# Gate and up weights: seven blocks, each in a tile of its own, split in the order of their products

## The chip, the cores and the metric

The kernel runs on one core of a Trainium2 chip. The metric is the device time of one execution in microseconds (us). Engines: TensorE (PE; its weight loads PEld), VectorE (DVE), ScalarE (ACT), GpSimd (POOL) and SyncE (SP, which issues the transfers).

## The reference

One layer of a hybrid decoder in fp32, on 1024 prompt positions and 64 sample positions (8 sequences of 8), 1088 columns in all:

```python
h = rms_norm(x, norm_mix_g)
proj = h @ w_in                       # convolution head group and dilated attention
x = x + concat([a, o]) @ w_out
h = rms_norm(x, norm_ffn_g)
g_full = concat([ffn_past, h @ w_ffn_gate])
g = depthwise_conv_valid(g_full, ffn_conv_w, ffn_conv_b)     # width 3
x = x + (silu(g) * (h @ w_ffn_up)) @ w_ffn_down
y = rms_norm(x, norm_final_g)
```

D_MODEL is 1024, D_FF is 2816. The change lies in the two products `h @ w_ffn_gate` and `h @ w_ffn_up`.

## The kernel before

Every matrix product is made exact by splitting both operands into a high part, which ACT writes by a copy that rounds to the matrix type, and a low part, the rest, which a subtraction writes (on POOL for the weights of this stage). Three matmuls then stand for one: high by high, high by low, low by high.

Gate and up are computed by a fast scheme for 2 x 2 blocks (Strassen and Winograd), seven products of blocks instead of eight. The inner dimension of 1024 is halved, the columns of h are halved (544 each), and a "weight" is a pair j of output tiles, j and j + 11, of 128 rows each. So a weight has four blocks of 128 x 512: a11 and a12 from the first output tile (raw tile g), a21 and a22 from the second (raw tile u), and four sums made of them:

- u2 = u1 + u2 gives s1, u1 = g1 - u1 gives s3, g1 = (new u2) - g1 gives s2, g2 = g2 - g1 gives s4. Here g1, g2, u1, u2 are halves of the raw tiles, and the sums (DVE, L945 to L948) are written in their place.

`products` multiplies the seven blocks with seven blocks of h (b11, t2, b21, t1, t3, b22, t4) in the order a11, s2, a12, s1, s3, s4, a22. Each product is 4 x 2 x 3 = 24 matmuls of 272 columns. Results accumulate in PSUM: px (a11, then a12), py (s2, then s1, then s4) and pz (s3, then a22). Between products DVE and ACT read them out: ta is a copy of px after a11, tb is py + ta, and `put` adds what belongs to each quarter of the result. So a later product on py has to wait for the sum read from it.

`ffn_pair(j)` does the gate of a pair, the width 3 convolution along columns (fc: one ACT and two DVE instructions per output tile, L1137 and L1139), the silu, then up, and u = up times the silu, which goes to DRAM in `ud`. There are eleven pairs; the first (gate0, up0) uses all eight products, without the scheme, while h is still being normalised, and takes its weights from splits of its own. Ten pairs, 20 weights, use the scheme.

Tiles for the weights of this stage:

- WR: two raw tiles of 1024 columns, filled by SP's transfers.
- WA: two tiles of 1024 columns, for the high and the low part of g (a11 and a12).
- W: five tiles of 1024 columns. `blocks_of_both` takes one for a22 (its high part in the left half, its low part in the right), two for s2 and s4 (high, low) and two for s3 and s1 (high, low).
- tmp: four tiles of 544 columns, used by ta and tb, and in the first pair by the sums that gate0 and up0 share.

What runs when is laid out by a planner at build time, from the order of the program, the free tiles and its own estimate of durations; at run time each engine goes through its instructions in the order laid out and waits where something is not ready.

After this stage, products with w_down follow (L172 to L174), which take their weights through the same WR and W tiles and read u back from DRAM.

Of the kernel before, what the change touches and what calls it, by code (L numbers as in the profile page):

```python
# [18 lines left out]
F32 = mybir.dt.float32  # L19
F32R = mybir.dt.float32r  # L20
AF = mybir.ActivationFunctionType
# [3 lines left out]
P = 128  # L25
D = 1024
# [38 lines left out]
HN = N // 2  # L65
# [12 lines left out]
def trunk_kernel(tc, xT, w_in, w_out, w_gate, w_up, w_down, par, kc, vc, sa, sf, pmask, smask,  # L78
                 yT, kT, vT, ca, cas, cf):
    nc = tc.nc  # L80
    with (
# [8 lines left out]
        def nm(s):  # L90
            cnt[0] += 1
            return f"{s}_{cnt[0]}"

        zone = {}
# [21 lines left out]
        def zt(z, tag, bufs, s, w=N, dt=F32):  # L116
            return zone[z].tile([P, w], dt, tag=tag, name=nm(s), bufs=bufs)

        def keep(s, w=N):
            return tp.tile([P, GW], F32, tag="T", name=nm(s))[:, :w]  # L120
# [143 lines left out]
        with ExitStack() as order:  # L264
            for k in range(KT):
                t = keep("x")
# [488 lines left out]
        i = 0  # L755
        for p in range(NS1, NP):
            prompt_heads(i, HEADS[p - NS1])
            i = HEADS[p - NS1]
# [55 lines left out]
        for p, upto in zip(range(NS1, NP), SHEADS):  # L814
            prompt_heads(i, upto)
            i = max(i, upto)
# [20 lines left out]
        def slot(tag, s, dt=F32R, w=HN):  # L837
            return zt("F", tag, 8, s, HN, dt)[:, :w]
# [43 lines left out]
        for h, tag in enumerate(("b11", "t2")):  # L882
            part.append([])
            for i in range(n):
                raw = slot("b11", "mx", F32)
                last_load = nc.sync.dma_start(raw, mixed[k0 + i][:, h * HN:h * HN + HN]).ins
                hi, lo = slot(tag, "mh"), slot(tag, "ml")
# [4 lines left out]
        for m0 in (0, 4):  # L892
            raw = wp.tile([P, D], F32, tag="WR", name=nm("wr"), bufs=WR)
            nc.sync.dma_start(raw.rearrange("p (m c) -> p m c", m=4),
                              w_out[m0:m0 + 4, :, k0 * P:].rearrange("m p c -> p m c"))
            for i in range(2):
                r = raw[:, i * 512:i * 512 + 512]
                hi, lo = slot("b21", "wh", w=512), slot("b21", "wl", w=512)
                nc.scalar.activation(hi, r, AF.Copy)
                nc.vector.tensor_sub(lo, r, hi.bitcast(F32))  # L900
                hi, lo = [t.rearrange("p (k c) -> p k c", c=P) for t in (hi, lo)]
# [14 lines left out]
        half = D // 2  # L916

        def weight_raw(w, j):
            raw = []
            for i in (j, j + HF):  # L920
                raw.append(wp.tile([P, D], F32, tag="WR", name=nm("wr"), bufs=WR))
                with tc.issue_after(last_load):
                    nc.sync.dma_start(raw[-1], w[i])
            return raw

        def weight_parts(x, new):
            n = x.shape[-1]
            hi, lo = new
            nc.scalar.activation(hi, x, AF.Copy)  # L929
            nc.gpsimd.tensor_sub(lo, x, hi.bitcast(F32))  # L930
            hi, lo = [t.rearrange("p (k c) -> p k c", c=P) for t in (hi, lo)]
            return [(hi[:, i:i + 4], lo[:, i:i + 4]) for i in range(0, n // P, 4)]

        def blocks_of_first(raw):
            return weight_parts(raw[0], [zt("F", "WA", 2, "wa", D, F32R) for _ in range(2)])

        def blocks_of_both(raw):
            def wide(s):
                return wp.tile([P, D], F32R, tag="W", name=nm(s))

            g, u = raw
            t = wide("w22")
            a22, = weight_parts(u[:, half:], (t[:, :half], t[:, half:]))
            g1, g2, u1, u2 = g[:, :half], g[:, half:], u[:, :half], u[:, half:]
            nc.vector.tensor_add(u2, u1, u2)  # L945
            nc.vector.tensor_sub(u1, g1, u1)
            nc.vector.tensor_sub(g1, u2, g1)
            nc.vector.tensor_sub(g2, g2, g1)  # L948
            s2, s4 = weight_parts(g, [wide("s24") for _ in range(2)])
            s3, s1 = weight_parts(u, [wide("s31") for _ in range(2)])  # L950
            return [a22, s1, s2, s3, s4]

        def weight_blocks(w, j):
            raw = weight_raw(w, j)
            return blocks_of_first(raw) + blocks_of_both(raw)


        raw = weight_raw(w_gate, 0)
        gate0 = blocks_of_first(raw) + weight_parts(raw[1], [wp.tile([P, D], F32R, tag="W", name=nm("wa"))
                                                             for _ in range(2)])  # L960
        raw = weight_raw(w_up, 0)
        up0 = []
        for i in range(2):
            up0 += weight_parts(raw[0][:, i * half:i * half + half], [slot("t4", "wa", w=half) for _ in range(2)])
        up0 += weight_parts(raw[1], [wp.tile([P, D], F32R, tag="W", name=nm("wa")) for _ in range(2)])


        x2d = [dp.tile([P, N], F32, name=f"x2d{m}") for m in range(KT)]
# [1 line left out]
        def out_half(h, hook):  # L970


            c = slice(h * HN, h * HN + HN)
            for m in range(KT):
                ps = pair()
                block_product(ps, wl[m], part[h], True)
                x = x2[m][:, c]
                added = nc.vector.tensor_add(x, all_of(ps), x).ins
                nc.sync.dma_start(x2d[m][:, c], x)
                s = slot("t1", "sq", F32)  # L980
                nc.scalar.activation(s, x, AF.Square)
                if m == 0:
                    acc = s
                else:
                    added = nc.vector.tensor_add(acc, s, acc).ins
                hook(m, added)
            return acc, added
# [8 lines left out]
        sq0, _ = out_half(0, lambda *_: None)  # L996
# [18 lines left out]
        def first_half(w, between=lambda: None, hook=lambda k, last: None):  # L1015

            a11, a12, a21, a22 = w
            o = pair("px"), pair("py")
            two_products(o, (a11, a21), blocks["b11"], True)
            shared = [zt("F", "tmp", 4, "ta", HN) for _ in o]  # L1020
            for t, ps in zip(shared, o):
                nc.scalar.activation(t, all_of(ps), AF.Copy)
            between()
            two_products(o, (a12, a22), blocks["b21"], False, hook)
            kept = [slot("t4", "c1", F32) for _ in o]
            for t, ps in zip(kept, o):
                nc.scalar.activation(t, all_of(ps), AF.Copy)
            return kept, shared

        def second_half(w):  # L1030
            a11, a12, a21, a22 = w
            o = pair("pv"), pair("pz")
            two_products(o, (a12, a22), blocks["b22"], True)
            two_products(o, (a11, a21), blocks["t1"], False)
            return o
# [11 lines left out]
        g1, g_shared = first_half(gate0, between, spread_second)  # L1047
# [4 lines left out]
        u1, u_shared = first_half(up0)  # L1052
# [4 lines left out]
        g2 = second_half(gate0)  # L1057
# [41 lines left out]
        W = GW - 2  # L1099
# [7 lines left out]
        def ffn_pair(j):  # L1107
# [17 lines left out]
            if j:  # L1125
                products(weight_blocks(w_gate, j), c11, put)
            else:
                for i in range(2):
                    nc.scalar.activation(gb[i][:, 2:2 + HN], g1[i], AF.Copy)
                    put(i, 1, g2[i], g_shared[i])  # L1130
# [35 lines left out]
            if j:  # L1166
                products(weight_blocks(w_up, j), u11, put_u)
                return
# [56 lines left out]
        w = []  # L1225
# [158 lines left out]
```

## Time and profile before

| | |
|---|---|
| three timed runs | 1415.96, 1424.79, 1425.14 us, median 1424.79 |
| profiled execution | 1418.49 us, span 1416.7 us |
| mean granted clock of TensorE | 0.983 |
| busy: PE, DVE, ACT, POOL | 95%, 60%, 36%, 31% of the span |
| gate and up | from about 640 to 1121 us of the span |

In rows of instructions: the line of the kernel, the engine, the operation, the tile written and the tiles read by their names, shapes, a count; behind the bar busy us and mean ns of one, behind the next the engine's idle time ahead of them and what ended it. `s<-wr,s` is a split of s2 with s4 or s3 with s1, `wa` one of a11 with a12, `w` one of a22. In rows of time: start, duration, the same names, and in brackets the idle time ahead and its releaser. In rows of waits: who waited for whom, us in total, times, the longest. PEclk is the share of full speed that was granted to TensorE.

### The profile page before, as it was taken

The page shows a single profiled execution, that of the slowest core. Times are in us where ns is not written, and L with a number is a line of the kernel's source. Part 1 is how long each engine was busy: PE and PEld are TensorE (multiplying, and loading weights), DVE is VectorE, ACT ScalarE, POOL GpSimd, SP SyncE. Part 2 cuts the span into 40 slices and gives each one's busy share as a digit, 9 for nine tenths or more (in the row PEclk, how much of TensorE's full clock was granted, in tenths as well). Part 3 has the DMA queues.
Part 4 walks back from the last instruction along what each step waited for, and adds up shares of the span by engine and source line. Part 5 has one row for each costly group of instructions (what it writes and reads, how often), then busy time and mean ns, then how long its engine had stood idle before and what let it go on. Part 6 is the DMA issues. An engine that isn't in the chain of part 4 may idle for free.

```text
span 1416.7 us, 24825 instructions
## 1 busy us (share of the span) xinstructions
PE 1351.9 (95%) x10059; PEld 1280.7 (90%) x10059; DVE 853.0 (60%) x1636; ACT 512.1 (36%) x984; POOL 436.5 (31%) x299
## 2 busy tenths in 40 slices
PE   6989999999999999979999999999999999999995
PEld 6989889999977777879999999999999889999995
DVE  7498695566574665598767565576555642323146
ACT  5312212457565564255333332233332331112033
POOL 3221112111000115131555554554554322224124
PEclk9999999999999999989999999999999999999998
DMA  7237676746699786350121221221222571414003
GB/s 274 62 133 262 224 257 202 205 143 172 190 282 244 235 230 226 118 191 1 63 92 46 76 92 62 92 74 48 92 75 79 186 277 54 131 49 132 12 16 112
DMA packets 84882, 195.16 MB, mean 138 GB/s; under 512 B 12576, under 2 KB 46752, under 8 KB 84768
## 3 DMA queue, kind: packets, MB, share of 16 engines
q1 hardware_dynamic: 84768, 193.57, 42.8%
q8 instruction: 79, 1.29, 0.4%
q14 instruction: 35, 0.29, 0.1%
HBM read 145.03 MB, written 48.52 MB: 137 GB/s over the span
## 4 chain that ended last, share of the span: by engine, by line
PE 74%; DVE 13%; DMA 4%; issue 3%; POOL 3%; ACT 1%; SPq 1%; POOLq 0%; DVEq 0%; ACTq 0%
PE g L172 10%; PE g L174 10%; PE g L173 10%; DVE cacc L342 4%; PE py L852 4%; PE py L849 4%; PE py L851 4%; PE o L675 3%; PE s L590 3%; PE t L658 3%; PE px L849 2%; PE px L852 2%; PE px L851 2%; PE pz L849 2%; PE pz L852 2%
## 5 line engine op out<-in xcount | busy, mean ns | idle before, releaser
L148 POOL TENSOR_TENSOR wl<-wr,wh 128x768 fp32r<-128x768 f32 (+2 forms) x61 | 116.4, 1909 | 457.6 <-PE g L174 373.6
L172 PE MATMUL g<-xh,wh 128*128 128x384 f32 (+1 forms) x472 | 157.5, 334 | 0.0
L174 PE MATMUL g<-xh,wl 128*128 128x384 f32 (+1 forms) x472 | 156.1, 331 | 0.0
L173 PE MATMUL g<-xl,wh 128*128 128x384 f32 (+1 forms) x472 | 156.1, 331 | 0.0
L172 PE MATMUL g<-ah,wh 128*128 128x384 f32 (+1 forms) x432 | 140.8, 331 | 4.2 <-ACT ah L1198 2.7
L173 PE MATMUL g<-al,wh 128*128 128x384 f32 (+1 forms) x432 | 142.9, 331 | 2.1 <-DVE al L1199 2.1
L174 PE MATMUL g<-ah,wl 128*128 128x384 f32 (+1 forms) x432 | 142.1, 331 | 0.7 <-POOL wl L148 0.7
L146 ACT ACTIVATE wh<-wr 128x768 fp32r<-128x768 f32 (+2 forms) x62 | 52.0, 839 | 237.5 <-PE g L174 176.1
L930 POOL TENSOR_TENSOR s<-wr,s 128x1024 fp32r<-128x1024 f32 x40 | 117.5, 2958 | 65.4 <-ACT s L929 62.8
L1221 DVE TENSOR_TENSOR x<-g,x 128x384 f32<-128x384 f32 (+1 forms) x72 | 38.0, 533 | 137.0 <-PE g L174 137.0
L1139 DVE SCALAR_TENSOR_TENSOR fc<-gb,prm,fc 128x1104 f32<-128x1104 f32 x44 | 97.8, 2243 | 8.8 <-ACT fc L1137 8.5
L631 ACT ACTIVATE y<-y,m 128x128 f32<-128x128 f32 (+1 forms) x192 | 88.4, 463 | 32.2 <-DVE m L619 32.1
L174 PEld LDWEIGHTS g<-xh,wl 128*128 128x128 f32 x472 | 89.1, 189 | 2.0 <-issue 1.8
L172 PEld LDWEIGHTS g<-xh,wh 128*128 128x128 f32 x472 | 89.2, 189 | 1.4 <-issue 1.2
L173 PEld LDWEIGHTS g<-xl,wh 128*128 128x128 f32 x472 | 89.2, 189 | 1.1 <-issue 1.0
L594 DVE CUSTOM_DVE_ANT_0 y<-s,pmk 128x128 f32<-128x128 f32 (+1 forms) x192 | 63.9, 378 | 40.9 <-PE s L590 33.3
L930 POOL TENSOR_TENSOR wa<-wr,wa 128x1024 fp32r<-128x1024 f32 (+1 forms) x25 | 59.6, 2389 | 91.3 <-ACT wa L929 87.5
L172 PEld LDWEIGHTS g<-ah,wh 128*128 128x128 f32 x432 | 81.4, 189 | 5.1 <-ACT ah L1198 3.1
L173 PEld LDWEIGHTS g<-al,wh 128*128 128x128 f32 x432 | 81.6, 189 | 3.0 <-DVE al L1199 3.0
L174 PEld LDWEIGHTS g<-ah,wl 128*128 128x128 f32 x432 | 81.5, 189 | 1.0 <-POOL wl L148 1.0
L342 DVE SCALAR_TENSOR_TENSOR cacc<-gp,prm,cacc 128x1024 f32<-128x1024 f32 x60 | 79.9, 1332 | 0.1
L390 DVE TENSOR_TENSOR qkv<-g,rb 128x384 f32<-128x384 f32 (+1 forms) x53 | 41.1, 776 | 46.0 <-PE g L174 45.9
(356 smaller groups left out, 4103.4 us busy)
## 6 DMA issues: line engine op xcount, KB each, us to landing
cr<-in_kc SPq DMA_DIRECT2D x24, 768.0 KB, 8.6
cr<-in_vc SPq DMA_DIRECT2D x24, 768.0 KB, 6.9
kk<-dk SPq DMA_DIRECT2D x48, 256.0 KB, 7.5
u<-u SPq DMA_DIRECT2D x22, 544.0 KB, 2.9
ur<-u SPq DMA_DIRECT2D x22, 544.0 KB, 5.0
wr<-in_w_in SPq DMA_DIRECT2D x22, 512.0 KB, 5.1
wr<-in_w_gate SPq DMA_DIRECT2D x22, 512.0 KB, 3.3
wr<-in_w_up SPq DMA_DIRECT2D x22, 512.0 KB, 4.3
```

The source lines that it names most:

```text
L148: lo_eng.tensor_sub(lo, raw, hi.bitcast(F32))
L172: nc.tensor.matmul(ps[c], whi[:, k, :], xh[:, t0:t0 + n], start=(k == 0), stop=False)
L173: nc.tensor.matmul(ps[c], whi[:, k, :], xl[:, t0:t0 + n], start=False, stop=False)
L174: nc.tensor.matmul(ps[c], wlo[:, k, :], xh[:, t0:t0 + n], start=False, stop=(k == nk - 1))
L342: eng.scalar_tensor_tensor(acc[:, :S], gp[:, j:j + S], col(w0 + j), acc[:, :S], op0=ALU.mult, op1=ALU.add)
L594: nc.vector.tensor_tensor_reduce(out=y[:, o:o + n], in0=ps[:, o:o + n], in1=mask, op0=ALU.add, op1=ALU.min, scale=1.0, scalar=3e38, accum_ ...
L631: nc.scalar.activation(y, y, AF.Exp, bias=m[:, 4 * g + i:4 * g + i + 1], scale=-1.0, accum_out=den[:, g, 2 * hd + u, i:i + 1])
L849: nc.tensor.matmul(ps, whi[:, k, :], xh[:, t], start=(start and k == 0), stop=False, skip_group_check=True)
L851: nc.tensor.matmul(ps, whi[:, k, :], xl[:, t], start=False, stop=False, skip_group_check=True)
L852: nc.tensor.matmul(ps, wlo[:, k, :], xh[:, t], start=False, stop=(k == nk - 1), skip_group_check=True)
L930: nc.gpsimd.tensor_sub(lo, x, hi.bitcast(F32))
L1139: nc.vector.scalar_tensor_tensor(c[:, :W], gb[i][:, t:t + W], col(C_FW + 3 * f + t), c[:, :W], op0=ALU.mult, op1=ALU.add)
```

## The change

Every one of the seven blocks of a weight gets a tile of its own with the high part in its left half and the low part in its right: a11 and a12 in the two WA tiles, s2, s1, s3, s4 and a22 in the five W tiles. Each is split by one ACT and one POOL instruction of 512 columns. The sum u1 + u2 goes to a tmp tile x instead of u2's place, so that a22 can be split last. Blocks are made in the order a11, a12, s2, s1, s3, s4, a22. gate0 and half of up0 get their blocks in the same way.

```diff
-        def blocks_of_first(raw):
-            return weight_parts(raw[0], [zt("F", "WA", 2, "wa", D, F32R) for _ in range(2)])
-
-        def blocks_of_both(raw):
-            def wide(s):
-                return wp.tile([P, D], F32R, tag="W", name=nm(s))
-
-            g, u = raw
-            t = wide("w22")
-            a22, = weight_parts(u[:, half:], (t[:, :half], t[:, half:]))
+        def block_tile(x, zone=False):
+
+            t = zt("F", "WA", 2, "wa", D, F32R) if zone else wp.tile([P, D], F32R, tag="W", name=nm("wb"))
+            hi, lo = t[:, :half], t[:, half:]
+            nc.scalar.activation(hi, x, AF.Copy)
+            nc.gpsimd.tensor_sub(lo, x, hi.bitcast(F32))
+            return [t.rearrange("p (k c) -> p k c", c=P) for t in (hi, lo)]
+
+        def plain_blocks(raw):
+            return [block_tile(r[:, i * half:i * half + half], r is raw[0]) for r in raw for i in range(2)]
+
+        def weight_blocks(w, j):
+
+            g, u = weight_raw(w, j)
             g1, g2, u1, u2 = g[:, :half], g[:, half:], u[:, :half], u[:, half:]
-            nc.vector.tensor_add(u2, u1, u2)
+            a11 = block_tile(g1, True)
+            a12 = block_tile(g2, True)
+            x = zt("F", "tmp", 4, "s1", HN)[:, :half]
+            nc.vector.tensor_add(x, u1, u2)
             nc.vector.tensor_sub(u1, g1, u1)
-            nc.vector.tensor_sub(g1, u2, g1)
+            nc.vector.tensor_sub(g1, x, g1)
+            s2 = block_tile(g1)
+            s1 = block_tile(x)
             nc.vector.tensor_sub(g2, g2, g1)
-            s2, s4 = weight_parts(g, [wide("s24") for _ in range(2)])
-            s3, s1 = weight_parts(u, [wide("s31") for _ in range(2)])
-            return [a22, s1, s2, s3, s4]
-
-        def weight_blocks(w, j):
-            raw = weight_raw(w, j)
-            return blocks_of_first(raw) + blocks_of_both(raw)
-
-        raw = weight_raw(w_gate, 0)
-        gate0 = blocks_of_first(raw) + weight_parts(raw[1], [wp.tile([P, D], F32R, tag="W", name=nm("wa"))
-                                                             for _ in range(2)])
+            s3 = block_tile(u1)
+            s4 = block_tile(g2)
+            a22 = block_tile(u2)
+            return [a11, a12, a22, s1, s2, s3, s4]
+
+        gate0 = plain_blocks(weight_raw(w_gate, 0))
         raw = weight_raw(w_up, 0)
         up0 = []
         for i in range(2):
             up0 += weight_parts(raw[0][:, i * half:i * half + half], [slot("t4", "wa", w=half) for _ in range(2)])
-        up0 += weight_parts(raw[1], [wp.tile([P, D], F32R, tag="W", name=nm("wa")) for _ in range(2)])
+        up0 += [block_tile(raw[1][:, i * half:i * half + half]) for i in range(2)]
```

## The prediction

> **What bounds the kernel now.** I read the page first, then the busy time by stretches of 100 us, to find the stage that the change touches (gate and up, 640 to 1121 us) and its limit.
>
> ```profile
> PE 1351.9 (95%) x10059; PEld 1280.7 (90%) x10059; DVE 853.0 (60%) x1636; ACT 512.1 (36%) x984; POOL 436.5 (31%) x299
> ...
> 600.00:640.00 40.00, 32.49 (x218) 31.81 (x218) 34.96 (x53) 19.82 (x31) 12.83 (x6) 0.85 0.53 183
> ...
> 800.00:900.00 100.00, 97.99 (x772) 96.80 (x772) 61.23 (x65) 31.94 (x36) 52.14 (x40) 1.00 0.22 76
> ...
> 1000.00:1100.00 100.00, 98.64 (x782) 97.75 (x781) 57.45 (x68) 31.36 (x35) 49.76 (x38) 1.00 0.21 72
> ```
>
> The columns of the last three rows are the stretch, its length, then busy us (and count) of PE, PEld, DVE, ACT and POOL, the granted clock, the DMA share and GB/s. In the stage PE is busy 98 to 99%, at a clock of 1.00; POOL, which makes every low part of the weights, is busy half of the time and ACT a third. So PE bounds the stage, and preparing weights can only give back the gaps between products. How large are they? I asked who PE waited for between 640 and 1130 us, and then looked at one pair (gate, then up) in order of time.
>
> ```profile
> PE py L852 <- POOL s L930: 4.6, 10, 0.7
> PE py L849 <- DVE u L1158: 2.4, 10, 0.3
> ...
> 799.15 0.28 PE L851 MATMUL px<-b11l,wa 128*128 128x272 f32 x1
> ...
> 799.78 0.29 PE L851 MATMUL pz<-t3l,s 128*128 128x272 f32 x1
> 800.51 0.39 PE L852 MATMUL py<-t2h,s 128*128 128x272 f32 x1 [0.44 <-POOL s L930]
> 800.75 0.29 PE L849 MATMUL py<-t2h,s 128*128 128x272 f32 x1
> ...
> 806.62 0.29 PE L851 MATMUL pz<-t3l,s 128*128 128x272 f32 x1
> 807.14 0.39 PE L849 MATMUL py<-t1h,s 128*128 128x272 f32 x1 [0.23 <-DVE u L1158]
> 807.37 0.29 PE L851 MATMUL py<-t1l,s 128*128 128x272 f32 x1
> ```
>
> Two waits, each once in every pair of weights, ten pairs. A busy matmul row lasts 0.29 us, but the pitch is what counts: from 799.15 to 799.78 five matmuls start, 0.126 us each. The first wait takes 799.78 to 800.51 (0.73) where 0.125 was due, and the next start is 0.24 later instead of 0.125: 0.605 + 0.115 = 0.72 us lost, more than the 0.44 that the row shows, since the weight load behind it is uncovered too. The second takes 0.52 and 0.23 where 0.125 was due twice: 0.50 us. Together 1.22 us in a pair, 12.2 in ten; the first pair's first wait is longer (the 0.7 in the list of waits), so 12.4 in all. The chain that ended last gives a check:
>
> ```profile
> 754.57 2.65 POOL s L930
> ...
> 1100.61 2.65 POOL s L930
> ```
>
> The same split starts eight pairs later 346.04 us on, 43.26 us for a pair; a pair has 2 x 7 x 4 x 2 x 3 = 336 matmuls, 42.0 us at 0.125, so 1.26 us is lost in a pair. Nothing else is to be had in the steady stage.
>
> Why are the waits there? The five W tiles come free after s3 (two, the high and low parts that s3 and s1 share), after s4 (two) and after a22 (one). The next weight takes a tile for a22 first, then two for s2 and s4, so its second product waits for a row of work: a22 split, four DVE sums, the split of s2 and s4. From the end of s3 to the start of the next s2 lie three products (s4, a22, a11) of 24 matmuls, 9.0 us; the row takes 0.63 + 1.29 + 4 x 0.69 + 1.05 + 2.65 = 8.4 us (rows here and below) and the gaps between engines. It is just in time, or just late.
>
> ```profile
> 791.22 1.28 POOL L930 TENSOR_TENSOR w<-wr,w 128x512 fp32r<-128x512 f32 x1 [2.92 <-ACT w L929]
> 792.54 0.69 DVE L945 TENSOR_TENSOR wr<-wr 128x512 f32<-128x512 f32 x1 [1.17 <-POOL w L930]
> ...
> 797.82 6.06 POOL L930 TENSOR_TENSOR s<-wr,s 128x1024 fp32r<-128x1024 f32 x2 [1.66 <-ACT s L929]
> ...
> 796.83 1.37 DVE L1139 SCALAR_TENSOR_TENSOR fc<-gb,prm,fc 128x1104 f32<-128x1104 f32 x1 [0.84 <-ACT fc L1137]
> 798.11 0.72 DVE L1120 TENSOR_TENSOR gb<-pz,gb 128x544 f32<-128x544 f32 x1
> 798.75 7.71 DVE L1139 SCALAR_TENSOR_TENSOR fc<-gb,prm,fc 128x1104 f32<-128x1104 f32 x3
> 806.37 0.72 DVE L1158 TENSOR_TENSOR u<-py,ta 128x544 f32<-128x544 f32 x1
> ...
> L1139 DVE SCALAR_TENSOR_TENSOR fc<-gb,prm,fc 128x1104 f32<-128x1104 f32 x36 | 81.4, 2279 | 7.9 <-ACT fc L1137 7.6
> ```
>
> The second wait is tied to the first. While POOL splits s2/s4 and s3/s1 (797.82 to 803.88), DVE's convolution steps take 7.71 us for three, against 1.37 for the one that ran before (2.28 on the mean, the last row); so the sum out of py (L1158) starts only at 806.37 and PE, which wants to add the next product to the same py, waits for it.
>
> **The change part by part.**
>
> *Splits in halves.* Per weight, four splits (1024, 512, 1024, 1024 columns) become seven of 512.
>
> ```profile
> L930 POOL TENSOR_TENSOR s<-wr,s 128x1024 fp32r<-128x1024 f32 x34 | 100.5, 2977 | 52.1 <-ACT s L929 52.1
> L930 POOL TENSOR_TENSOR wa<-wr,wa 128x1024 fp32r<-128x1024 f32 x17 | 40.9, 2404 | 66.1 <-ACT wa L929 66.1
> L930 POOL TENSOR_TENSOR w<-wr,w 128x512 fp32r<-128x512 f32 x17 | 21.9, 1288 | 42.6 <-ACT w L929 42.6
> ...
> L929 ACT ACTIVATE s<-wr 128x1024 fp32r<-128x1024 f32 x34 | 34.0, 1048 | 39.0 <-DVE wr L948 39.0
> L929 ACT ACTIVATE wa<-wr 128x1024 fp32r<-128x1024 f32 x17 | 17.9, 1052 | 52.9 <-PE px L851 33.4 <-DMA wr<-in_w_up 19.5
> L929 ACT ACTIVATE w<-wr 128x512 fp32r<-128x512 f32 x17 | 10.8, 634 | 68.1 <-PE pz L851 34.7 <-issue 33.4
> ```
>
> POOL now: 2 x 2.98 + 2.40 + 1.29 = 9.65 us; then 7 x 1.29 = 9.0 us (more where DVE is in its way, at most 7 x 1.49 = 10.4 at the s rows' rate). ACT: 2 x 1.05 + 1.05 + 0.63 = 3.78, then 7 x 0.63 = 4.44: 0.66 us more per weight, 13 us over 20 weights. Neither is on the path: a weight lasts 21.6 us, and ACT's idle two thirds cover it. If that cover were gone, the 13 us would show.
>
> [...]
>
> *Order and tiles.* Both parts of a block share one tile, and W tiles come free after s2, s1, s3, s4 and a22, one each; the next weight takes them in that same order. So s2 has a tile from the present weight's second product on, six products (18 us) ahead; then its load sets it. With loads landed by 806 (below), two splits of a11 and a12, a sum and its own split follow (2 x 1.29 + 0.69 + 0.63 + 1.29 behind each other, 5.2 us): ready near 812, needed 21.6 us behind 799.4, at 821. The first wait goes: -0.72 a pair. The last split, a22, waits for the end of the weight before and is needed six products later.
>
> *x in a tile of its own.* u1 + u2 goes to one of the four tmp tiles, of which ta and tb use two, so the sums need not wait for a22's split (the wait of L945, 1.17 us above, off the path). With x, three of four are in use: cost nothing. In the first pair after the start four are held by the shared sums of the opening; they come free before the first of these weights' second product, so a few us at most, once.
>
> *Where POOL then works.* With s2, s1, s3 and s4 split during the previous weight, only a22 (1.29 us) falls on the time right behind a gate's end. The three convolution steps would take 3 x 1.37 + 1.29 = 5.4 instead of 7.71, and the sum of L1158 starts 2.3 us sooner. PE asks for it 0.72 sooner than now, and it was 0.5 late: 1.1 us to spare. The second wait goes: -0.50 a pair. No row shows POOL's new places; from both sides, this term is 0.50 gained, or (contention stays) 0.72 lost, since PE arrives sooner at the same late sum. I take the gain, the nearer to the row of 1.37.
>
> *Loads.* The raw tiles come free after the splits of s4 and a22, rather than after s2/s4 and s3/s1.
>
> ```profile
> ACT w L929 <- PE pz L851: 38.9, 10, 4.2
> ...
> ACT wa L929 <- DMA wr<-in_w_up: 19.5, 3, 7.0
> ...
> 800.49 3.75 SPq L923 DMA_DIRECT2D wr<-in_w_gate  x2
> ...
> wr<-in_w_gate SPq DMA_DIRECT2D x22, 512.0 KB, 3.3
> wr<-in_w_up SPq DMA_DIRECT2D x22, 512.0 KB, 4.3
> ```
>
> Now both loads issue from 800.49 on, 2.4 us behind the sum out of the gate's last product (798.11), 3.75 us for the two, and land after a median of 3.3 to 4.3. Afterwards g's is free when s4 is split, a product earlier, and u's 1.92 us (0.63 + 1.29) behind the gate's last product, by about 800: landed by 805 or 806. ACT met such a load late three times, and a tile late ten times, and PE did not. Behind the loads in SP's queue are only the stores of u. No cost.
>
> *Opening and end.* gate0 and up0 get three more splits, 0.7 us of ACT, which is idle half of 600 to 640. After the last product the chain is the store and reload of u:
>
> ```profile
> 1126.89 9.85 DMA ur<-u
> 1136.76 1.12 ACT ah L1198
> ...
> 1100.00:1150.00 50.00, 43.77 (x284) 41.80 (x283) 32.09 (x30) 18.27 (x19) 13.99 (x6) 0.97 0.75 269
> ```
>
> It moves along unchanged. Sum: -12.4 us (7.3 and 5.1) on an execution of 1418.49 us (span 1416.7): 1406.1. The three timed runs are 1415.96, 1424.79 and 1425.14, median 6.3 above it; the same step from their median gives 1412, which I forecast.
>
> **The rivals.** *The wait moves to DVE.* If splits still lie on the convolution steps, the sum out of py stays as late, and what PE gains on s2 it loses there: between 0 and -6 us, 1419 to 1425. For it: the order on the engines is laid out by a planner, and POOL has 9 us of splits in each 21.6. Against: s2 no longer has to come there. Chance 0.22.
>
> *DVE waits for a load (slower).* Today the first instruction that meets a late load is ACT's split of wa, which waited up to 7.0 us with no harm to PE. Now the sum into x has no split ahead of it; if the planner puts it on DVE at the load's planned landing and the load is late, all sums out of PSUM queue behind it. Between the product s2 and the product s1 on the same py lie 3.0 us, the sum takes 0.72, so 2.3 us of lateness are free; beyond that PE stands. At 0.62 us past this in each of 20 weights the gain is used up; at 1.2 us in each it is 24 - 12 = +12, 1437. For it: three such waits in the list; against: 17 weights without one. Chance 0.13.
>
> *More than the sum.* PE idles 6 us between 1100 and 1150 and 7.5 between 600 and 640; shorter POOL instructions may shorten the DVE queue at the stage's end too: -18, 1406. Chance 0.15.
>
> **How the numbers follow.** Forecast 0.50, 9 to 15 us gained. The range goes from 1400 (the forecast on the fastest run shown, 1403.6, and most of the third rival) to 1430 (no gain at all and the mild part of the slower case); 0.08 is left above, 0.09 below. About 1% is what a measurement here can tell from no change, 14 us; the forecast lies just inside. Faster by over 1%: the third rival and a quarter of the forecast, 0.15 + 0.12 = 0.27. Slower: 0.11 of the second. Within: 0.62.
>
> **What would show it.** The waits of PE for POOL s and DVE u are gone from the list between 640 and 1130, and a pair lasts 42.0 to 42.3 us. Seven splits of 512 per weight, 1.3 to 1.5 us each; fc below 1.9 us on the mean (2.28 in the steady stage now). The first rival shows as PE waiting for DVE u over 1 us a pair; the second as DVE waiting for wr. I am wrong, too, if the planner lays out another order of products, with gaps that no row here has.

## The result and the profile after

| | before | after |
|---|---|---|
| median of the timed runs | 1421.51 us (1415.96 to 1432.4, 19 runs) | 1410.53 us (1404.5 to 1419.07, 19 runs) |
| ratio | | 0.9918, 95% interval 0.9903 to 0.9932 |
| profiled execution, span, clock | 1418.49, 1416.7 us, 0.983 | 1410.36, 1408.6 us, 0.982 |

The kernel is faster by 0.8%, 11.7 us. The forecast was 1412. The first line is the busy time of each engine on the page, the second the stretch of the changed stage (length, then busy us and count of PE, PEld, DVE, ACT, POOL, then the granted clock):

```profile
PE 1348.9 (96%) x10059; PEld 1282.0 (91%) x10059; DVE 844.7 (60%) x1636; ACT 521.9 (37%) x1047; POOL 447.0 (32%) x362
...
640.00:1130.00 490.00, 486.20 (x3816) 484.65 (x3815) 309.58 (x375) 183.21 (x262) 246.29 (x230) 0.99 0.24 82
```

The matmuls are the same 10059. ACT and POOL have 63 instructions more each (three for each of the 20 weights, three in the opening) and some ten us more of work; DVE has 8 us less with the same 1636 instructions.

The list of PE's waits between 640 and 1130 us after the change is complete here:

```profile
PE g L173 <- DVE al L1203: 1.5, 1, 1.5
PE py L849 <- DVE gb L1124: 0.9, 1, 0.9
PE g L172 <- ACT ah L1202: 0.8, 1, 0.8
PE g L172 <- DVE u L1162: 0.6, 1, 0.6
```

Both waits that came ten times are gone. Three of the four lines belong to the w_down products behind the stage; one, on L849, is new and comes once. Then the pitch of a pair, from the first matmul of s2's product in the first pair of the scheme that runs evenly and the same one nine pairs later, in PE's order of time:

```profile
718.10 0.29 PE L849 MATMUL py<-t2h,wb 128*128 128x272 f32 x1
...
1096.56 0.29 PE L849 MATMUL py<-t2h,wb 128*128 128x272 f32 x1
```

378.46 / 9 = 42.05 us, against 43.26. That is the 336 matmuls at 0.125 us, and PE has nothing left to win here.

Where the 8.1 us between the two profiled executions lie follows from four marks on PE. Each row is an interval between first matmuls:

| interval, us | before | after | difference |
|---|---|---|---|
| last half of the out products (mh) to the first product on px | 38.12 | 37.98 | -0.1 |
| to the first s2 product of the scheme | 56.00 | 57.15 | +1.2 |
| s2 to the first w_down matmul: the ten pairs | 429.77 | 418.65 | -11.1 |
| to the end of the span | 295.3 | 294.0 | -1.3 |

So the change did its work in the ten pairs, -11.1 us. The 1.2 us of the second row are pace and not a wait: 28 of its 408 matmuls start about 0.23 us apart instead of 0.125, against 17 before, and the other profiles of this study have 16 to 29 there, kernels with the change and without it. The 1.3 us of the last row aren't clear of scatter either, since it runs from 292.9 to 297.0 in the other profiles. The profiled difference is smaller than -11.1, namely -8.1, mainly because the first mark itself came 3.3 us later in this execution (600.81 against 597.5 us). It lies between 597.5 and 607.3 in the profiles of this study, and the splits that were edited all run behind it.

One pair, in order of time, on DVE, POOL and PE. The gate's last matmul starts at 799.80:

```profile
799.36 1.97 DVE L1143 SCALAR_TENSOR_TENSOR fc<-gb,prm,fc 128x1104 f32<-128x1104 f32 x1 [1.44 <-ACT fc L1141]
801.26 0.71 DVE L1124 TENSOR_TENSOR gb<-pz,gb 128x544 f32<-128x544 f32 x1
801.89 5.79 DVE L1143 SCALAR_TENSOR_TENSOR fc<-gb,prm,fc 128x1104 f32<-128x1104 f32 x3
807.60 0.71 DVE L1162 TENSOR_TENSOR u<-py,ta 128x544 f32<-128x544 f32 x1
```

```profile
797.63 2.54 POOL L939 TENSOR_TENSOR wb<-wr,wb 128x512 fp32r<-128x512 f32 x2
800.12 1.26 POOL L1138 COPY cfo<-gb 128x2 f32<-128x2 f32 x1
801.48 1.29 POOL L939 TENSOR_TENSOR wb<-wr,wb 128x512 fp32r<-128x512 f32 x1
805.23 1.29 POOL L939 TENSOR_TENSOR wa<-wr,wa 128x512 fp32r<-128x512 f32 x1
```

```profile
799.80 0.29 PE L852 MATMUL pz<-t4h,wb 128*128 128x272 f32 x1
...
809.33 0.29 PE L849 MATMUL py<-t1h,wb 128*128 128x272 f32 x1
```

The three convolution steps take 5.79 us instead of 7.71. The sum out of py is done at 808.31 and PE asks for it at 809.33: 1.02 us to spare, where before it was done at 807.09 and PE started at 807.14, held by it. POOL still works while the steps run, on a22 and on a11 of the next weight, and the first step (1.97 instead of 1.37) lies beside the end of the splits of s3 and s4.

The groups of instructions from 740 to 1100 us, by shape:

```profile
L939 POOL TENSOR_TENSOR wb<-wr,wb 128x512 fp32r<-128x512 f32 x69 | 92.0, 1344 | 47.6 <-ACT wb L938 47.6
L939 POOL TENSOR_TENSOR wa<-wr,wa 128x512 fp32r<-128x512 f32 x34 | 43.9, 1291 | 78.9 <-ACT wa L938 78.9
L1143 DVE SCALAR_TENSOR_TENSOR fc<-gb,prm,fc 128x1104 f32<-128x1104 f32 x36 | 68.6, 1924 | 13.3 <-ACT fc L1141 13.0
L938 ACT ACTIVATE wb<-wr 128x512 fp32r<-128x512 f32 x68 | 42.8, 629 | 145.2 <-DVE wr L954 91.7 <-PE py L852 26.2 <-PE pz L852 19.4
```

### The profile page after: what moved, and what is told of

It reads as the page before. It is cut to its first block, busy times and chain, and to the rows that moved or that the text cites. A ratio compares the mean times of both kernels' runs of the same rounds, so it can differ in the third digit from the quotient of the medians.

```text
span 1408.6 us, 25028 instructions
## 1 busy us (share of the span) xinstructions
PE 1348.9 (96%) x10059; PEld 1282.0 (91%) x10059; DVE 844.7 (60%) x1636; ACT 521.9 (37%) x1047; POOL 447.0 (32%) x362
## 3 DMA queue, kind: packets, MB, share of 16 engines
q8 instruction: 79, 1.29, 0.4%
## 4 chain that ended last, share of the span: by engine, by line
PE 76%; DVE 10%; issue 5%; DMA 5%; POOL 2%; ACT 1%; SPq 1%; POOLq 0%; DVEq 0%; ACTq 0%
PE g L174 10%; PE g L172 10%; PE g L173 10%; PE py L849 4%; PE py L851 4%; PE py L852 4%; DVE cacc L342 4%; PE o L675 3%; PE s L590 3%; PE pz L852 3%; PE pz L849 3%; PE pz L851 3%; PE px L849 3%; PE px L852 3%; PE px L851 3%
## 5 line engine op out<-in xcount | busy, mean ns | idle before, releaser
L939 POOL TENSOR_TENSOR wb<-wr,wb 128x512 fp32r<-128x512 f32 x84 | 115.2, 1383 | 56.8 <-ACT wb L938 56.8
L938 ACT ACTIVATE wb<-wr 128x512 fp32r<-128x512 f32 x84 | 52.4, 628 | 164.2 <-DVE wr L954 105.0
L1143 DVE SCALAR_TENSOR_TENSOR fc<-gb,prm,fc 128x1104 f32<-128x1104 f32 x44 | 83.5, 1918 | 14.7 <-ACT fc L1141 14.4
L939 POOL TENSOR_TENSOR wa<-wr,wa 128x512 fp32r<-128x512 f32 x42 | 54.9, 1308 | 101.0 <-ACT wa L938 101.0
```

Of the source, the lines that this page charges most:

```text
L1143: nc.vector.scalar_tensor_tensor(c[:, :W], gb[i][:, t:t + W], col(C_FW + 3 * f + t), c[:, :W], op0=ALU.mult, op1=ALU.add)
```

## The experiments

Ratios are to the kernel before, run beside each. "Fill" below is the number of matmuls of s3 that PE does ahead of s1's product, beside the 24 of a12 that always stand there (in the kernel before, two of the five lie inside s2's product), so that PE has work while the sum out of py is made. "Sum done" and "s1 starts" are us behind the gate's end (its last matmul's start + 0.12), in the one pair near 800 us. "Pair" is the period of the even pairs, and the mean of fc is that of 740 to 1100 us.

| kernel | ratio, 95% interval | pair, us | sum done, s1 starts | fill | fc mean, us |
|---|---|---|---|---|---|
| before | 1 | 43.26 | 9.71, 9.75 | 5 | 2.25 |
| after (again) | 0.9923 (0.9901 to 0.9946) | 42.05 | 8.40, 9.41 | 9 | 1.96 |
| halves alone | 0.9931 (0.9913 to 0.9950) | 42.03 | 9.66, 9.89 | 13 | 2.05 |
| x apart alone | 0.9931 (0.9910 to 0.9951) | 42.07 | 7.79, 9.67 | 13 | 1.75 |
| own tiles, old sums and order | 0.9937 (0.9913 to 0.9961) | 42.06 to 42.3, one of 43.16 | 7.75, 9.41 | 11 | 1.77 |
| s3 ahead of s1 alone | 0.9911 (0.9882 to 0.9939) | 42.04 | 8.62, 9.25 | 24 | 1.79 |
| before, no fill | 1.0099 (1.0069 to 1.0129) | 44.66 | 9.56, 9.62 | 0 | 2.25 |
| halves, no fill | 0.9931 (0.9903 to 0.9959) | 42.27 | 8.38, 8.63 | 0 | 1.95 |
| after, no fill | 0.9923 (0.9897 to 0.9948) | 42.13 | 8.54, 8.63 | 0 | 1.99 |
| after, extra POOL work meant for the steps | 0.9927 (0.9901 to 0.9952) | 42.05 | 7.92, 9.40 | 9 | 1.78 |
| after, extra POOL work elsewhere | 0.9934 (0.9908 to 0.9959) | 42.05 | 8.47, 9.40 | 9 | 1.98 |
| after, no low parts | 0.9881 (0.9853 to 0.9908) | 42.05 | 6.30, 9.39 | 9 | 1.37 |
| after, s3 ahead of s1 | 0.9903 (0.9880 to 0.9927) | 42.01 | 4.95, 9.0 | 24 | 1.99 |

### Which part takes the waits away

The first four ran beside each other: the changed kernel once more, and three kernels that each do one part of the change.

> The changed kernel once more, as the measure for the three kernels beside it. Both theories: ratio to the kernel before 0.990 to 0.994, no wait of PE for POOL or DVE in the steady stage, a pair 42.05 us.

Measured: 1411.76 us, and the stages of the table above to 0.5 us (ten pairs 418.66).

**Halves alone.**

```diff
-            nc.scalar.activation(hi, x, AF.Copy)
-            nc.gpsimd.tensor_sub(lo, x, hi.bitcast(F32))
+            for i in range(0, n, half):
+                c = slice(i, min(i + half, n))
+                nc.scalar.activation(hi[:, c], x[:, c], AF.Copy)
+                nc.gpsimd.tensor_sub(lo[:, c], x[:, c], hi[:, c].bitcast(F32))
```

> The kernel before with every split of 1024 columns made as two of 512, same tiles, same order. Theory (the two waits are tied: the sum out of py is late because splits lie on the convolution steps, whatever PE does before): s2's low part comes 1.3 us sooner, so the wait for POOL goes (from 4.6 us to under 1), but PE then waits about 1 us a pair for DVE; in all 0 to -3 us, ratio 0.998 to 1.0. Rival A (the gain comes from short splits alone): ratio 0.992, both waits gone. Rival B (each wait goes by itself): -7 us, ratio 0.995.

Measured: 1411.48 us, all of the gain, and no wait of PE at all from 690 to 1110 us. My theory had the second wait stay; it fell. But DVE's order of time shows that the sum isn't sooner:

```profile
801.34 0.72 DVE L1122 TENSOR_TENSOR gb<-pz,gb 128x544 f32<-128x544 f32 x1 [1.25 <-PE pz L852]
801.98 8.18 DVE L1141 SCALAR_TENSOR_TENSOR fc<-gb,prm,fc 128x1104 f32<-128x1104 f32 x4
810.08 0.72 DVE L1160 TENSOR_TENSOR u<-py,ta 128x544 f32<-128x544 f32 x1
```

All four steps now follow the gate's last sum, 8.18 us, and the sum out of py is done 9.66 us behind the gate's end, as in the kernel before (9.71). What differs is PE: the planner put 13 matmuls of s3 ahead of s1's product instead of 5, one more microsecond of work. So an edit of the splits moved PE's order too.

**x in a tile of its own,** with a22 split first and s24, s31 as before:

```diff
-            nc.vector.tensor_add(u2, u1, u2)
+            x = zt("F", "tmp", 4, "s1", HN)[:, :half]
+            nc.vector.tensor_add(x, u1, u2)
...
-            nc.vector.tensor_sub(g1, u2, g1)
+            nc.vector.tensor_sub(g1, x, g1)
...
-            s3, s1 = weight_parts(u, [wide("s31") for _ in range(2)])
+            hi, lo = [wide("s31") for _ in range(2)]
+            s3, = weight_parts(u1, (hi[:, :half], lo[:, :half]))
+            s1, = weight_parts(x, (hi[:, half:], lo[:, half:]))
```

> The kernel before with u1 + u2 in a tmp tile, so that the sums need not wait for the split of a22; tiles shared in twos and a22 first, as before. Theory: the row ahead of s2 is 2 to 3 us shorter, the wait for POOL goes; the splits of s2 and s4 leave the convolution steps in part, so 5 to 10 us gained, ratio 0.993 to 0.9965. Rival (tiles of their own are needed): s2 still just in time, ratio 0.999 to 1.0.

Measured: 1411.02 us, pair 42.07. The waits of the even pairs are gone, some 2 us remain in the first pair.

**Own tiles, with the sums in place and a22 split first:**

```diff
+            a11 = block_tile(g1, True)
+            a12 = block_tile(g2, True)
+            a22 = block_tile(u2)
...
+            s2 = block_tile(g1)
+            s1 = block_tile(u2)
...
+            s3 = block_tile(u1)
+            s4 = block_tile(g2)
```

> The changed kernel with the sums in place again and so a22 split first; every block keeps a tile of its own. Theory (what counts is that a tile comes free after every product, so that nothing is made just in time and few splits lie on the convolution steps): as the changed kernel within 3 us, ratio 0.990 to 0.994, pair 42.0 to 42.3. Rival (the order of the splits is what counts): the waits come back, ratio 0.997 to 1.0.

Measured: 1410.81 us. Again the whole gain by the time. The profile is a little less even than the theory had it: three single waits of 0.6 to 0.8 us come back, two in the first pair and one in a later pair of 43.16 us, and the ten pairs take 421.35 us against 418.66. Three different edits each give what the whole change gives, and the intervals hold each other's values. The two waits were 0.7 and 0.5 us of lateness in a pair that PE fills from end to end: whoever removes that much lateness gets all there is, and a second edit finds nothing left.

### Is it the planner's fill?

Halves alone left the sum as late and gained through the order on PE. The next four, side by side, test that: s3's product swapped with s1's (24 matmuls of fill, splits and tiles of the kernel before), and s3's product bound behind s1's (no fill of s3) in three kernels.

```diff
+            block_product(z, s3, blocks["t3"], True)
             block_product(y, s1, blocks["t1"], False)
...
-            block_product(z, s3, blocks["t3"], True)
```

> The kernel before with nothing changed but the order of two products: s3 ahead of s1. The planner puts 19 matmuls of a12 into s2 as well. Theory (what counts is that PE has other matmuls to do where a block or a sum is late): both waits go, ratio 0.990 to 0.994, with splits and tiles as before. Rival (the splits have to come sooner): at least the wait for POOL stays, ratio 0.995 to 1.0.

Measured: 1410.84 us, pair 42.04, no wait of PE from 690 to 1110 us. POOL's splits are still of 1024 columns:

```profile
802.89 2.42 POOL L930 TENSOR_TENSOR s<-wr,s 128x1024 fp32r<-128x1024 f32 x1 [3.30 <-PE py L852]
...
806.01 2.41 POOL L930 TENSOR_TENSOR s<-wr,s 128x1024 fp32r<-128x1024 f32 x1 [0.45 <-PE pz L852]
```

The swap of two lines does what the change does. s2 isn't late either, though its splits are no faster: the first begins 2.8 us ahead of the gate's end (805.70) instead of 0.4 behind it. Part of that is the gate's end itself, ahead of which the planner now put all 24 matmuls of a11 instead of 8. It also put 19 matmuls of a12 into s2's product.

The other three share this edit, where `done` is the last matmul of s1's product:

```diff
-            block_product(y, s1, blocks["t1"], False)
+            done = block_product(y, s1, blocks["t1"], False)
...
-            block_product(z, s3, blocks["t3"], True)
+            with tc.issue_after(done):
+                block_product(z, s3, blocks["t3"], True)
```

On the kernel with halves alone:

> The kernel before with splits in halves (as e1), and s3's product issued only after s1's, so that PE has nothing of s3 to put between s2 and s1. Theory (the second wait is hidden by matmuls of s3, 13 of them here in up where the kernel before had 5; the sum out of py is as late as before, done 9.66 us behind the gate's end): PE asks for it 8.27 us behind the gate's end, so about 1.4 us are lost in a pair, PE waits for DVE near 1.2 us ten times, and the time is 10 to 15 us above e1's, ratio 1.000 to 1.005. Rival (short splits free DVE and that is the gain): as e1, ratio 0.991 to 0.995.

Measured: 1414.35 us, 0.9931. The gain stays without any fill, so fill isn't the whole cause. The planner had laid out DVE differently as well, with one step ahead of the gate's last sum:

```profile
799.15 1.37 DVE L1143 SCALAR_TENSOR_TENSOR fc<-gb,prm,fc 128x1104 f32<-128x1104 f32 x1
800.44 0.72 DVE L1124 TENSOR_TENSOR gb<-pz,gb 128x544 f32<-128x544 f32 x1
801.07 6.41 DVE L1143 SCALAR_TENSOR_TENSOR fc<-gb,prm,fc 128x1104 f32<-128x1104 f32 x3
```

Three steps take 6.41 us and the sum is done at 8.38 instead of 9.66. PE isn't held by it: 21 matmuls of a11, 24 of s2 and 24 of a12 stand ahead, 69 x 0.125 = 8.63, and at 8.63 it starts, not at the 8.27 that was expected. The 0.2 us that are lost in a pair (42.27) come at the third matmul of s1's product, the first that needs the low part, which POOL has ready only at 808.63:

```profile
808.36 0.29 PE L849 MATMUL py<-t1h,s 128*128 128x272 f32 x1
808.49 0.28 PE L851 MATMUL py<-t1l,s 128*128 128x272 f32 x1
808.68 0.39 PE L852 MATMUL py<-t1h,s 128*128 128x272 f32 x1
```

```profile
806.31 2.32 POOL L933 TENSOR_TENSOR s<-wr,s 128x512 fp32r<-128x512 f32 x1
```

On the changed kernel:

> The changed kernel with s3's product issued only after s1's. Its sum out of py was done 8.4 us behind the gate's end, and PE now asks for it at 8.27: 0.1 to 0.3 us lost in a pair, 1 to 3 us in all, ratio 0.992 to 0.995. If the fill is all that counts: as e9, ratio 1.000 to 1.005; if the fill counts for nothing: 0.9918, no wait at all.

Measured: 1413.65 us, 0.9923, pair 42.13. Here, too, PE comes at 8.63 and finds the sum done at 8.54. A longer wait is in the first pair, the only one from 690 to 1110 us, and that pair takes 47.95 us against 43.20:

```profile
PE py L849 <- DVE gb L1126: 3.0, 1, 3.0
```

On the kernel before:

> The kernel before with s3's product issued only after s1's; the planner then puts 21 matmuls of a12 into s2, ahead of its late low part. Theory: the wait for POOL goes, the sum out of py is done 9.7 us behind the gate's end and PE asks at 8.27: 1.5 us lost in a pair against 1.22 before, so 0 to +5 us, ratio 1.000 to 1.004, all of it PE waiting for DVE. Rival (each wait by itself): the wait for POOL goes and 5 to 7 us with it, ratio 0.995 to 0.9965.

Measured: 1438.92 us, 1% slower, more than any theory said. The planner had put 21 matmuls of a12 inside the gate's s2 product, and three products then waited for their sums in nearly every pair:

```profile
PE py L849 <- DVE u L1160: 4.3, 9, 0.5
PE px L849 <- ACT ta L1083: 4.2, 9, 0.5
PE py L849 <- DVE gb L1122: 4.1, 8, 0.5
```

With the fill taken from all three, the sum is done at 9.56 (splits of 1024), 8.38 (halves) and 8.54 (the change), and PE, unhindered, comes at 8.63: only the kernel before is late. In all three DVE's order is the same, one step ahead of the gate's last sum and three behind it; the three take 7.59 us with splits of 1024 and 6.41 with halves. So halving the splits does by itself bring the sum about 1.2 us sooner there. The kernels before and after differ by 9.71 - 8.39 = 1.3. In the change the splits are shorter and also lie elsewhere, and how the 1.3 divides between the two, these runs don't part.

### POOL beside the convolution steps

Four subtractions of 256 columns per output tile on POOL, written between the steps:

```diff
+                for k in range(4 if j else 0):
+                    d = gb[i][:, 2:258] if i else gb[i][:, 600:856]
+                    nc.gpsimd.tensor_sub(zt("F", "dummy", 1, "dum", 256), d, d)
```

> The changed kernel with eight extra subtractions of 256 columns on POOL in each pair, from a result of the gate into a tile that nothing reads, laid on the convolution steps; PE's order of products is that of the changed kernel. Theory (two-input work of POOL slows DVE's convolution steps, and the sum out of py with them): the steps take 2 to 3 us more, the sum is done 2 to 3 us later where 1.0 is to spare, PE waits for DVE u 1 to 2 us a pair; 10 to 20 us above the changed kernel, ratio 0.999 to 1.006. Rival (POOL's place is of no account, as the kernel with halves alone suggests): as the changed kernel, ratio 0.990 to 0.994.

Measured: 1412.62 us, as the changed kernel, against a theory that had it lose. DVE and POOL near 805 us:

```profile
804.99 5.32 DVE L1146 SCALAR_TENSOR_TENSOR fc<-gb,prm,fc 128x1104 f32<-128x1104 f32 x3
810.23 0.71 DVE L1165 TENSOR_TENSOR u<-py,ta 128x544 f32<-128x544 f32 x1
```

```profile
804.44 0.61 POOL L1144 TENSOR_TENSOR dum<-gb 128x256 f32<-128x256 f32 x1
805.15 2.35 POOL L939 TENSOR_TENSOR wb<-wr,wb 128x512 fp32r<-128x512 f32 x1
807.47 1.68 POOL L1144 TENSOR_TENSOR dum<-gb 128x256 f32<-128x256 f32 x1
```

Of the eight extra subtractions in a pair only one lay wholly on the three steps (the one at 807.47); one ended as they began, and the others came at their end or later. So the edit put far less beside the steps than it was meant to, and its theory is hardly tested. Where the two engines met, both lost: a split took 2.35 instead of 1.29 us and the subtraction 1.68 instead of 0.61, and the three steps took 5.32, less than in the changed kernel (5.79) but more than the 4.1 that they take without any split beside them (below).

The same work placed elsewhere, behind the gate's a12, as the control:

```diff
+                for k in range(8):
+                    d = gb[0][:, 2 + k % 2 * 256:258 + k % 2 * 256]
+                    nc.gpsimd.tensor_sub(zt("F", "dummy", 1, "dum", 256), d, d)
```

> The same eight subtractions in each pair, laid behind the gate's a12 product, where DVE has little to do; PE's order again that of the changed kernel. Theory: no cost, ratio 0.990 to 0.994, no waits of PE. Rival (POOL's load as such is what counts): as the kernel with them on the convolution steps.

Measured: 1413.68 us, as said, but for the one wait of 0.9 us in the first pair that the changed kernel has as well. The control isn't clean, since one of its eight subtractions lay on the first step. The pair of runs doesn't show what POOL beside the steps costs: one subtraction lay there in either, and PE has 1 us to spare.

POOL's splits of the seven blocks away, the high part standing in for the low one:

```diff
-            nc.gpsimd.tensor_sub(lo, x, hi.bitcast(F32))
-            return [t.rearrange("p (k c) -> p k c", c=P) for t in (hi, lo)]
+            return [t.rearrange("p (k c) -> p k c", c=P) for t in (hi, hi)]
```

> The changed kernel without POOL's splits of the seven blocks: the high part stands in for the low part in the third matmul, so the low parts of the weights are left out of the products; PE's work and order are the same. Theory (the change has taken all that weights can give back, PE bounds the stage): within 3 us of the changed kernel, ratio 0.990 to 0.994, pair 42.0 us; the three convolution steps take 1.3 to 1.4 us each. Rival (splits still cost something): 5 us or more below it, ratio under 0.989.

Measured: 1405.81 us. The steps run at their own speed, 1369 ns by the group of 740 to 1100 us,

```profile
L1142 DVE SCALAR_TENSOR_TENSOR fc<-gb,prm,fc 128x1104 f32<-128x1104 f32 x36 | 49.3, 1369 | 15.0 <-ACT fc L1140 14.6
```

and the pair is 42.05 us still: in the even stage, weights that cost POOL nothing at all are worth nothing more than the change. The time is the rival's all the same, 5 to 6 us below the changed kernel, though the two intervals overlap. Most of it is in the opening, which the theory had left out: 34.64 us instead of 37.98 in the first row of the table of stages, 55.56 instead of 57.15 in the second; the one wait in the first pair is gone as well (417.52 for the ten pairs). The stretch of 600 to 640 us, first of the changed kernel, then of this one:

```profile
600.00:640.00 40.00, 31.01 (x213) 30.14 (x213) 32.39 (x49) 20.65 (x36) 12.56 (x8) 0.88 0.55 191
```

```profile
600.00:640.00 40.00, 34.15 (x244) 33.47 (x245) 32.78 (x57) 21.23 (x37) 3.05 (x2) 0.91 0.56 191
```

DVE does 57 instructions instead of 49, though in this execution the opening also began 2.1 us sooner, and PE's wait for DVE's sum of squares fell from 3.7 to 1.8 us. So DVE is on the path there, and POOL's splits cost something: at most the 4.9 us of the two rows. About 2.2 of them are matmuls that start 0.23 us apart, 31 instead of 53 in the two rows, a number that goes from 36 to 55 in the other profiles. I tried no order that avoids it.

### Both cures together

The changed kernel with s3 ahead of s1 (the swap above):

> The changed kernel with the product s3 ahead of s1, as in the kernel that changes that order alone. The steady stage has nothing left to give; the one wait of 0.9 us in the first pair goes: 0 to 2 us below the changed kernel, ratio 0.9895 to 0.993. If the two gains added up: 0.983.

Measured: 1408.99 us, 0.9903. If the gains added up, it would be 0.983, which the interval excludes. It isn't to be told from the change or from the swap alone. The wait in the first pair went, as expected, but one of 0.9 us came in the last pair, for the sum tb; a pair takes 42.01 us.

## Why the prediction was right

- **The bound.** Right. PE at 0.125 us a matmul is all of a pair, 42.05 against 42.0, and no experiment went below 42.01.
- **The two waits.** Right: both lines are gone, and the pair fell by 1.21 us where 1.22 was summed and 42.0 to 42.3 forecast.
- **The sum.** -12.4 forecast; -11.1 in the ten pairs, -11.7 by the ratio (-9.7 to -13.8). Nearly all of the missing 1.3 is one wait in the first pair, which takes 43.20 us instead of 42.05.
- **The first pair.** "A few us at most, once" was said of the tmp tiles and left out of the sum; it should have been a term. What came is this. DVE's order of time has no gap from 697.08 us on, and two of its instructions in there are long (the L1174 at 701.26 takes 0.71, the L1153 of the same shape at 700.56 takes 0.64):

```profile
698.19 1.81 DVE L1174 TENSOR_TENSOR u<-c,fc 128x544 f32<-128x544 f32 x1
...
701.89 1.75 DVE L1153 TENSOR_TENSOR u<-u,fc 128x480 f32<-128x480 f32 x1
...
704.33 0.71 DVE L1124 TENSOR_TENSOR gb<-py,ta 128x544 f32<-128x544 f32 x1
```

```profile
695.96 3.46 POOL L939 TENSOR_TENSOR wb<-wr,wb 128x512 fp32r<-128x512 f32 x2 [0.60 <-ACT wb L938]
...
701.59 1.53 POOL L939 TENSOR_TENSOR wa<-wr,wa 128x512 fp32r<-128x512 f32 x1 [1.53 <-ACT wa L938]
```

```profile
705.10 0.39 PE L849 MATMUL py<-t1h,wb 128*128 128x272 f32 x1 [0.85 <-DVE gb L1124]
```

  Each ran while POOL split a block, and each took 1.1 us more; the sum that PE waits for is last in this queue. Without low parts the wait is absent. So the two long rows are enough to account for the 1.1 us lost. The tile of x isn't needed for such a wait: the kernel with own tiles and the sums in place has none, and waits there too (0.8 and 0.6 us). Whether it adds to this one, no run separates.
- **Shorter POOL work beside DVE.** Right in direction, too large in size. Three steps were to fall from 7.71 to 5.4 and took 5.79; the sum was to come 2.3 us sooner and came 1.3, since the first step also lay beside splits (1.97). fc was to be below 1.9 us on the mean and is 1.92; the splits take 1.29 to 1.34 on the mean, as said. s2's low part was to be ready 9 us ahead of its product and is ready 5.9 us ahead near 800 us (796.28 for 802.18), early enough either way.
- **The spare time.** 1.1 forecast, 1.02 found, but by another way: PE did not ask 0.72 us sooner, since the planner put six more matmuls ahead of s1, four of s3 and two of a11. The sum came 1.0 us later than forecast and PE 0.9 later: two errors cancelled, and that the figure fits is luck.
- **That the second wait is tied to the first,** and so stays as long as the sum out of py is late (the theory for halves alone): not so. Halves alone, x alone, own tiles alone or the swap each removed both.
- **The rivals.** No wait moved to DVE: the list has no line for DVE u L1162 on py. No DVE wait for a load either. ACT met the late load more often, nine times rather than three, and it cost PE nothing:

```profile
ACT wa L938 <- DMA wr<-in_w_up: 30.5, 9, 4.3
```

  "More than the sum" did not come: the opening kept its length (37.98 against 38.12), and the 1.3 us at the end are within the scatter of that row.

What stays open: every edit also made the planner lay out PE and DVE anew (fill of 0, 5, 9, 11, 13 and 24 matmuls, the first step ahead of the gate's last sum or behind it), so the share of the shorter splits, the free tiles and the new order in the change itself can't be parted. Only the total is shown.

## What to carry to other kernels

Before an edit is priced by its parts, compare the period of the steady stage with its bound, here 43.26 us with 336 x 0.125 = 42.0: the difference is all that any edit can give there, and the cheapest one that removes the lateness takes it all (here a swap of two products did as much as new tiles, splits and order together, and two cures didn't add up). Where a planner lays out the order, look at what it did to every engine after each edit before a gain is put down to the line edited.

## What the runs showed of the hardware that I had not expected

I took it that DVE pays whenever POOL works beside it. Three convolution steps without POOL's splits take 4.1 us (3 x 1369 ns). With splits of 1024 columns beside them they took 7.71, with 512 columns 5.79 to 6.41, and with one of 512 and a subtraction of 256 they took 5.32. POOL's own instructions stretched as well, 1.29 to 2.35 and 0.61 to 1.68 us in that last run. The cleanest comparison is the pair without fill, where DVE's order is the same and the splits of s2, s4, s3 and s1 are two of 1024 columns or four of 512. DVE's loss on the three steps fell from 3.5 to 2.3 us (7.59 and 6.41 against 4.1), and POOL's on these splits rose from 1.2 (6.04 against 2 x 2.41) to 3.7 (8.86 against 4 x 1.29). So with shorter splits more of the loss fell on POOL there; the other kernels also differ in how much POOL does beside the steps.

Which of the two lost more was not the same everywhere. In the first pair POOL's splits were under way (from 695.96 and from 701.59) when the two long DVE instructions came (698.19, 701.89). These took 1.1 us more each, and the split from 701.59 took 0.24 us more (1.53 against 1.29). In the run with extra subtractions DVE's step had begun (804.99) when the split came (805.15), and the split took 1.06 us more. What decides it, no run here shows.
